# The dt projection as one 48-column stationary, laid out again by selection matmuls

## The chip, the cores and the metric

The kernel runs on one core of one Trainium2 chip. A core has five engines that work side by side and wait for each other only through semaphores: TensorE (PE in the profile, its weight loads PEld), VectorE (DVE), ScalarE (ACT), GpSimd (POOL) and SyncE (SP), which here issues DMAs. Times are microseconds of one execution on the device, from three timed runs; a separate profiled execution gives the trace.

## The reference

The reference is one layer of a hybrid decoder on 512 positions of width 1024: a mixer (16 Mamba-2 SSD heads of dimension 64 and pooled channel groups that share one input projection), cross-attention into 256 memory tokens, and a SwiGLU network, each behind an RMS norm. Only the head's step sizes matter here, all in float32:

```
proj = rmsnorm(x) @ w_in
z, xbc, dt_raw, v = split(proj)                 # dt_raw: 512 positions x 16 heads
dt   = softplus(dt_raw + dt_bias)
adt  = dt * (-exp(a_log))                       # per chunk of 128 positions, 4 chunks
a_cs = cumsum(adt, within the chunk)
seg  = exp(a_cs[l] - a_cs[s])  where l >= s     # in y_diag = (C B^T * seg) (xs * dt)
decay_states = exp(a_cs[last] - a_cs)           # states = B^T (decay_states * xs * dt)
chunk_decay  = exp(a_cs[last])                  # carries the state from chunk to chunk
```

Each position of a head thus needs three numbers: `dt`, `a_cs`, and `dt * decay_states`, the last two once the running sum of the chunk is there.

## The kernel before

Activations lie transposed, features on the 128 partitions and the 512 positions along the free dimension. A projection works on weight units of 128x1024 floats (eight blocks of 128x128 for one block of 128 output features). Each float32 operand is split into a high part, rounded to the format in which TensorE multiplies in one pass (ACT, `whi`, `t_xgh`, `t_uh`), and the low rest (DVE, `wlo`, `t_xgl`, `t_ul`); a product is three matmuls, high by high, high by low, low by high (`mm3`, lines 117 to 119). SP loads the units from HBM into six buffers (`raw`), ACT casts them into four (`whi`), DVE subtracts into five (`wlo`). A cast of a new unit therefore waits for the last matmul that reads the unit four earlier.

`SPEC` is a list of slots; a slot's items issue their matmuls together, with the preparation of the next slot, the follow-up of the slot before, and the casts of coming weights around them. In the first slot (`i_start`) all orders are those of the text; from the second slot on, the framework's scheduler fixes the order of every engine's instructions when the program is built. Engines execute in that order, so an instruction that waits holds up all that stand behind it on its engine.

The first slot projects the raw input, scaled by the norm's gain, for the step sizes (unit 0, PSUM tile `s`) and two blocks of convolution channels (units 1 and 2, also `s`); string `START_MM` lists them as unit and k-block. Token `r` in it is the matmul of the sum of squares (`r<-t_xacc,ones`, line 301), after which the norm's factor `t_r1t` is computed and the projections are multiplied by it.

For `dt` the 16 columns of the weight stand three times in a block of 96 (at 0, 32 and 64), so that the projection comes out three times on PSUM partitions 0 to 95. `i_dt` runs the whole chain on 96x512: Abs, Exp, Ln for softplus (lines 428 to 446), the multiplication by minus `exp(a_log)`, and one scan over 512 positions (line 450) whose multiplier `smask` is zero at the start of each chunk. Rows 32 to 47 of the scan go to DRAM (`d_acs`), from where each head's row is later read back to all partitions (`t_abc`, `t_E`); the four last values of each head go out as `d_last` and come back broadcast as `dl`, of which ACT makes `decb`, the chunk decays. Three copies (`dt`, `a_cs`, and the product with the decay) are gathered in `t_Tt` and turned by four transposes of 96x128 in item `tk` (`tokT`), which gives `tok`, positions on partitions.

Other items the text speaks of: `n:k` makes the normalised input's block k (`t_x`, then `t_uh` and `t_ul`), needed from `x:6` and `z:0` on; `x` and `z` are projections (matmuls into `xbc` and `z`; conv taps in `t_cv`); `t:g.c` transposes convolved channels (`xst`) and multiplies them by `dt` (`t_xc`) and by the decayed `dt` (`t_xd`), each split into high (`t_xch`, `t_xdh`, ACT) and low; `s:g.c` multiplies `t_xd` by the transposed B (`t_btmh`) into the state of a chunk (`st`).

Of the kernel before, what the change touches and what calls it, by code (L numbers as in the profile page):

```python
# [61 lines left out]
def hybrid_block(ctx: ExitStack, tc: tile.TileContext, a: dict, out: bass.AP,  # L62
# [185 lines left out]
    add_unit("dt", a["w_dt"], KT * 96)  # L248
# [90 lines left out]
    def i_start(its):  # L339
        it = Item(keys=["dt"] + [k for i in its[1:] for k in i.keys])  # L340

        def prep():
# [16 lines left out]
            for kind, i in [(t[0], int(t[1])) for t in start.split()]:  # L359
# [4 lines left out]
                elif kind in "hH":  # L364
# [7 lines left out]
                    split_into(hi[:, c], lo[:, c], raws[i][:, c])  # L372
# [7 lines left out]
        def mm():  # L380
# [37 lines left out]
    def i_dt():  # L418
        it = Item()

        def post():
            yield from need("r1")
            ps = it.ps
            r = st["r1",]
            R = slice(0, 96)
            bias = col(V_DTB, R)
            xr = T("dtx")
            nc.vector.tensor_tensor(out=xr[R], in0=ps[R], in1=r[R], op=ALU.mult)
            ax = T("dta")
            nc.scalar.activation(ax[R], xr[R], AF.Abs, bias=bias)  # L430
            nc.vector.tensor_scalar(out=xr[R], in0=xr[R], scalar1=bias, scalar2=0.0, op0=ALU.add, op1=ALU.max)
            e = T("dte")
            nc.scalar.activation(e[R], ax[R], AF.Exp, scale=-1.0)
            na = SM("na", [P, 1])
            nc.scalar.activation(na[R], col(V_ALOG, R), AF.Exp)
            yield
            u = T("dtu")
            nc.vector.tensor_scalar(out=u[R], in0=e[R], scalar1=1.0, scalar2=None, op0=ALU.add)
            l = T("dtl")
            nc.scalar.activation(l[R], u[R], AF.Ln)  # L440
            yield
            nc.vector.scalar_tensor_tensor(out=e[R], in0=u[R], scalar=1.0, in1=e[R],
                                           op0=ALU.subtract, op1=ALU.subtract)
            nc.vector.tensor_tensor(out=l[R], in0=l[R], in1=e[R], op=ALU.subtract)
            dt = T("dt")
            nc.vector.tensor_tensor(out=dt[R], in0=l[R], in1=xr[R], op=ALU.add)
            adt = T("adt")
            nc.vector.tensor_scalar(out=adt[R], in0=dt[R], scalar1=na[R], scalar2=-1.0, op0=ALU.mult, op1=ALU.mult)
            acs = T("acs")
            nc.vector.tensor_tensor_scan(acs[R], smask[R], adt[R], 0.0, ALU.mult, ALU.add)  # L450
            d_acs = dram.tile([H, S], F32, name="d_acs")
            d_last = dram.tile([H, NC], F32, name="d_last")
            last = SM("last", [P, NC])
            nc.vector.tensor_copy(last[R], acs[R].rearrange("p (c l) -> p c l", l=P)[:, :, P - 1])
            nc.sync.dma_start(d_acs, acs[32:48, :])
            nc.sync.dma_start(d_last, last[32:48, :])
            st["d_acs"] = d_acs
            dl = const.tile([P, H * NC], F32, name="dl")
            nc.sync.dma_start(dl, d_last.rearrange("h c -> (h c)").unsqueeze(0).broadcast_to([P, H * NC]))
            decb = const.tile([P, H, NC], F32, name="decb")  # L460
            yield
            Tt = T("Tt")
            nc.scalar.copy(Tt[0:32], dt[0:32])
            nc.scalar.copy(Tt[32:64], acs[32:64])
            ex = T("ex")
            for c in range(NC):
                cs = slice(c * P, (c + 1) * P)
                nc.scalar.activation(ex[64:96, cs], acs[64:96, cs], AF.Exp, scale=-1.0,
                                     bias=last[64:96, c:c + 1])
            nc.vector.tensor_tensor(out=Tt[64:96], in0=ex[64:96], in1=dt[64:96], op=ALU.mult)  # L470
            st["decay"] = decb, dl.rearrange("p (h c) -> p h c", c=NC)
            st["Tt"] = Tt

        it.post = post
        return it

    def i_tok():
        it = Item()

        def mm():  # L480
            pt = hold(it, "tokT")
            for c in range(NC):
                nc.tensor.transpose(pt[:, c * 96:(c + 1) * 96], st["Tt"][0:96, c * P:(c + 1) * P],
                                    ident[0:96, 0:96])

        def post():
            tok = const.tile([P, NC, 96], F32, name="tok")
            nc.vector.tensor_copy(tok.rearrange("p c h -> p (c h)"), it.ps[:, 0:NC * 96])
            st["tok"] = tok
# [72 lines left out]
    def i_tokens(g, c):  # L562
# [8 lines left out]
        def post():  # L571
# [5 lines left out]
            for key, off in zip(keys, (0, 64)):  # L577
# [933 lines left out]
```

## Time and profile before

| | |
|---|---|
| three timed runs | 794.51, 794.70, 795.65 us |
| median | 794.7 us |
| span of the profiled execution (first to last instruction) | 793.5 us |
| median less that span | 1.2 us |
| mean granted TensorE clock | 0.996 |
| idle time of DVE, ACT in the span | 20%, 37% |

The profiled execution is told by its span alone; what lies around it is taken from the difference to the median. In a row of a timeline stand the start, the duration, the engine, the line of the kernel, the operation, what it writes and reads, its shape and count, and in brackets the idle time before it and what ended that. Matmuls overlap in the pipeline: a duration of 0.39 us with the next start 0.23 us later costs 0.23 us. A matmul of true float32 operands, whose rows have no high or low part in their names, is recorded as two instructions, a transpose as one.

### The profile page before, as it was taken

The page shows a single profiled execution, that of the slowest core. Times are in us where ns is not written, and L with a number is a line of the kernel's source. Part 1 is how long each engine was busy: PE and PEld are TensorE (multiplying, and loading weights), DVE is VectorE, ACT ScalarE, POOL GpSimd, SP SyncE. Part 2 cuts the span into 40 slices and gives each one's busy share as a digit, 9 for nine tenths or more (in the row PEclk, how much of TensorE's full clock was granted, in tenths as well). Part 3 has the DMA queues.
Part 4 walks back from the last instruction along what each step waited for, and adds up shares of the span by engine and source line. Part 5 has one row for each costly group of instructions (what it writes and reads, how often), then busy time and mean ns, then how long its engine had stood idle before and what let it go on. Part 6 is the DMA issues. An engine that isn't in the chain of part 4 may idle for free.

```text
span 793.5 us, 10440 instructions
## 1 busy us (share of the span) xinstructions
PE 782.1 (99%) x3780; PEld 655.1 (83%) x3780; DVE 635.8 (80%) x945; ACT 498.4 (63%) x799; POOL 49.9 (6%) x66
## 2 busy tenths in 40 slices
PE   9999999999999999999999999999999999999995
PEld 7888888888888888888888888888888888888984
DVE  7999879999885799875766667788867698868897
ACT  8667699557953547555655695665445575455845
POOL 0000000000000000000000001011101011101000
PEclk9999999999999999999999999999999999999998
DMA  9235225133475234775446268688879697869602
GB/s 331 91 112 184 109 82 179 54 111 122 162 257 171 84 107 150 170 198 163 134 116 153 60 154 222 171 243 166 239 157 291 163 251 172 245 154 272 165 14 106
DMA packets 41282, 128.60 MB, mean 162 GB/s; under 512 B 4864, under 2 KB 7296, under 8 KB 41232
## 3 DMA queue, kind: packets, MB, share of 16 engines
q1 hardware_dynamic: 33024, 99.30, 37.0%
q0 software_dynamic: 8064, 28.58, 20.1%
q8 instruction: 29, 0.48, 0.2%
q14 instruction: 21, 0.17, 0.1%
q10 hardware_dynamic: 144, 0.07, 0.1%
HBM read 116.63 MB, written 2.13 MB: 150 GB/s over the span
## 4 chain that ended last, share of the span: by engine, by line
PE 92%; DVE 5%; issue 1%; DMA 1%; ACT 0%; SPq 0%; DVEq 0%
PE gA L1102 15%; PE gB L1102 8%; PE dA L1102 5%; PE gC L1102 4%; PE dB L1102 2%; PE xbc L117 2%; PE xbc L119 2%; PE xbc L118 2%; PE vAB L1102 2%; PE k L889 2%; PE z L117 2%; PE z L119 2%; PE op L117 2%; PE z L118 2%; PE wo L119 2%; PE op L118 2%
## 5 line engine op out<-in xcount | busy, mean ns | idle before, releaser
L203 ACT CAST whi<-raw 128x1024 fp32r<-128x1024 f32 (+1 forms) x125 | 129.0, 1040 | 91.1 <-PE wo L118 11.8
L205 DVE TENSOR_TENSOR wlo<-raw,whi 128x1024 fp32r<-128x1024 f32 (+1 forms) x125 | 149.8, 1208 | 28.2 <-ACT whi L203 27.3
L203 ACT CAST whi<-wq 128x1024 fp32r<-128x1024 f32 (+1 forms) x76 | 77.4, 1028 | 74.6 <-PE dA L1102 17.8
L205 DVE TENSOR_TENSOR wlo<-wq,whi 128x1024 fp32r<-128x1024 f32 (+1 forms) x76 | 90.3, 1194 | 38.7 <-ACT whi L203 38.6
L172 POOL DMA_DIRECT2D raw<-w_s x38 | 32.8, 867 | 646.0 <-DMA raw<-w_s 486.4
L1102 PE MATMUL gA<-whi,t_xh 128*128 128x512 f32 (+1 forms) x192 | 71.8, 374 | 0.0
L1102 PE MATMUL gA<-wlo,t_xh 128*128 128x512 f32 (+1 forms) x192 | 71.4, 372 | 0.0
L1102 PE MATMUL gA<-whi,t_xl 128*128 128x512 f32 (+1 forms) x192 | 71.3, 371 | 0.0
L1102 PEld LDWEIGHTS gA<-whi,t_xh 128*128 128x128 f32 x192 | 36.2, 188 | 6.6 <-ACT whi L203 0.4
L1102 PEld LDWEIGHTS gA<-wlo,t_xh 128*128 128x128 f32 x192 | 36.2, 188 | 6.3
L1102 PEld LDWEIGHTS gA<-whi,t_xl 128*128 128x128 f32 x192 | 36.2, 188 | 6.1
L1118 ACT ACTIVATE t_gu<-t_gu,s 128x512 f32<-128x512 f32 (+1 forms) x24 | 16.4, 688 | 35.9 <-DVE t_gu L1114 35.8
L194 DVE TENSOR_TENSOR wq<-wq,wq 128x1024 f32<-128x1024 f32 (+1 forms) x19 | 22.5, 1194 | 17.7 <-DMA wq<-raw 17.7
L1102 PE MATMUL dA<-whi,t_xh 128*128 128x512 f32 x88 | 34.1, 392 | 0.3 <-DVE t_hT L1259 0.2
L1102 PE MATMUL dA<-whi,t_xl 128*128 128x512 f32 x88 | 34.3, 389 | 0.0
L1102 PE MATMUL dA<-wlo,t_xh 128*128 128x512 f32 x88 | 34.1, 389 | 0.0
L1102 PE MATMUL gB<-whi,t_xq 128*128 128x512 f32 (+1 forms) x96 | 27.5, 371 | 0.0
L1180 ACT CAST t_xh<-t_x 128x512 fp32r<-128x512 f32 x30 | 18.6, 621 | 10.6 <-DVE t_x L1199 6.4
L117 PE MATMUL wo<-t_oh,whi 128*128 128x512 f32 x64 | 25.2, 394 | 0.0
L117 PE MATMUL v<-t_uh,whi 128*128 128x512 f32 x64 | 25.1, 392 | 0.0
L117 PE MATMUL z<-t_uh,whi 128*128 128x512 f32 x64 | 25.1, 392 | 0.0
L117 PE MATMUL q<-t_hgh,whi 128*128 128x512 f32 x64 | 25.1, 392 | 0.0
(401 smaller groups left out, 2221.2 us busy)
## 6 DMA issues: line engine op xcount, KB each, us to landing
raw<-w_u SPq DMA_DIRECT2D x68, 512.0 KB, 3.4
raw<-w_s SPq DMA_DIRECT2D x54, 512.0 KB, 4.6
wq<-w_s SPq DMA_DIRECT2D x36, 512.0 KB, 5.9
raw<-w_s POOLq DMA_DIRECT2D x36, 512.0 KB, 7.5
wq<-raw POOLq DMA_DIRECT2D x17, 512.0 KB, 8.6
t_x<-xT SPq DMA_DIRECT2D x16, 256.0 KB, 5.4
t_abc<-d_acs SPq DMA_DIRECT2D x16, 256.0 KB, 4.6
out<-t_hT SPq DMA_DIRECT2D x8, 256.0 KB, 2.3
```

The source lines that it names most:

```text
L117: nc.tensor.matmul(ps, whi, xhi, start=start, stop=False)
L118: nc.tensor.matmul(ps, whi, xlo, start=False, stop=False)
L119: nc.tensor.matmul(ps, wlo, xhi, start=False, stop=stop)
L172: nc.gpsimd.dma_start(sw[c, f][:, :n], quad("11" if f == 7 else "22"), accum_op=ALU.add)
L194: add = nc.vector.tensor_tensor(out=sw[c, 3][:, :n], in0=sw[c, 3][:, :n], in1=sw[c, 6][:, :n], op=ALU.add)
L203: nc.scalar.copy(hi[:, :n], raw[:, :n])
L205: nc.vector.tensor_tensor(out=lo[:, :n], in0=raw[:, :n], in1=hi.bitcast(F32)[:, :n], op=ALU.subtract)
L889: nc.tensor.matmul(it.ps[d], wh[:, ws], both, start=k == 0, stop=False, skip_group_check=True)
L1102: nc.tensor.matmul(it.ps[tt], p[:, ts_], w[:, ws], start=first, stop=(c, i, n) == pairs[-1] and p is xh and w is wl, skip_group_check=True)
L1118: st["silu"] = nc.scalar.activation(g, g, AF.Silu, scale=st["r3",][:, c:c + 1])
L1180: nc.scalar.copy(h if w is None else h[:, w], src)
```

## The change

The weight of `dt` becomes a block of 48 columns: the high part at columns 0 to 15, the low part at 32 to 47, zeros between. Two passes, with the high and the low part of the input, then form all four products; their results lie on PSUM partitions 0 to 15 and 32 to 47. The first multiplication by `t_r1t` stays where it was (`t_dtx`, now 48x512). A new item `ds`, in a slot of its own after `x:3`, adds the two groups of rows and spreads the chunks over the partitions: for each chunk one float32 matmul with a 48x128 matrix of zeros and ones (`pick`, made on POOL), so that heads of chunk c stand on partitions 32c to 32c+15 and positions within the chunk along the free dimension (`dts`, 128x128). The chain for softplus, scan and decay runs on 128x128; the scan needs no restarts. `d_last` is now one value for each of 128 partitions, `d_acs` is written in four pieces, `dl` is 128x128. Three transposes of 128x128 give `tok`, whose indices change with the users of `tok` and `decb`. The mask `smask`, the copies into `t_Tt` and the copy `last` go.

```diff
-    "x:2", "x:3 n:0 n:1 n:2 n:3", "x:4", "n:4 n:5 n:6", "n:7", "x:5 z:0", "x:8 x:6",
+    "x:2", "x:3 n:0 n:1 n:2 n:3", "ds", "x:4", "n:4 n:5 n:6", "n:7", "x:5 z:0", "x:8 x:6",
...
-    smask = T("smask")
-    nc.gpsimd.memset(smask, 1.0)
-    nc.gpsimd.memset(smask.rearrange("p (c l) -> p c l", l=P)[:, :, 0:1], 0.0)
+    pick = T("pick").rearrange("p (c r) -> p c r", r=P)
+    nc.gpsimd.memset(pick, 0.0)
+    for c in range(NC):
+        for base in (0, 32):
+            nc.gpsimd.affine_select(out=pick[:, c, 32 * c:32 * c + H], in_=pick[:, c, 32 * c:32 * c + H],
+                                    compare_op=ALU.not_equal, fill=1.0, base=-base, pattern=[[-1, H]],
+                                    channel_multiplier=1)
...
-                    split_into(hi[:, c], lo[:, c], raws[i][:, c])
+                    if i == 0:
+                        nc.scalar.copy(hi[:, c], raws[i][:, c])
+                        h3 = hi[:, c].rearrange("p (k n) -> p k n", n=48)
+                        nc.vector.tensor_tensor(out=h3[:, :, 32:48],
+                                                in0=raws[i][:, c].rearrange("p (k n) -> p k n", n=48)[:, :, 32:48],
+                                                in1=h3.bitcast(F32)[:, :, 0:H], op=ALU.subtract)
+                    else:
+                        split_into(hi[:, c], lo[:, c], raws[i][:, c])
...
-                n = (96, P, P)[u]
+                n = (48, P, P)[u]
                 whi, wlo = ready[it.keys[u]]
+                if u == 0:
+                    for h in range(2):
+                        nc.tensor.matmul(pss[u][0:n, :], whi[:, k * n:(k + 1) * n], st["xg"][k][h],
+                                         start=k == 0 and h == 0, stop=k == KT - 1 and h == 1)
+                    continue
...
+    def i_dtsum():
+
+        it = Item()
+
+        def mm():
+            ps = hold(it, "dts")
+            for c in range(NC):
+                nc.tensor.matmul(ps[:, 0:P], pick[0:48, c, :], st["dtx"][0:48, c * P:(c + 1) * P],
+                                 start=c == 0, stop=c == NC - 1)
+
+        def post():
+            ps = it.ps[:, 0:P]
+            bias = col(V_DTB)
+            t = T("dta"), T("dtu")
+            ax, e, xr, u = [t[0][:, o:o + P] for o in range(0, 512, P)]
+            l, adt, ex, one = [t[1][:, o:o + P] for o in range(0, 512, P)]
+            nc.vector.memset(one, 1.0)
+            nc.scalar.activation(ax, ps, AF.Abs, bias=bias)
+            nc.vector.tensor_scalar(out=xr, in0=ps, scalar1=bias, scalar2=0.0, op0=ALU.add, op1=ALU.max)
+            nc.scalar.activation(e, ax, AF.Exp, scale=-1.0)
...
+            nc.vector.tensor_scalar(out=u, in0=e, scalar1=1.0, scalar2=None, op0=ALU.add)
+            nc.scalar.activation(l, u, AF.Ln)
...
+            nc.vector.tensor_scalar(out=adt, in0=dt, scalar1=na, scalar2=-1.0, op0=ALU.mult, op1=ALU.mult)
+            nc.vector.tensor_tensor_scan(acs, one, adt, 0.0, ALU.mult, ALU.add)
+            last = acs[:, P - 1:P]
+            d_acs = st["d_acs"] = dram.tile([H, S], F32, name="d_acs")
+            d_last = dram.tile([P, 1], F32, name="d_last")
+            nc.sync.dma_start(d_last, last)
             for c in range(NC):
+                nc.sync.dma_start(d_acs[:, c * P:(c + 1) * P], acs[32 * c:32 * c + H])
+            dl = T("dl", n=P).rearrange("p (c h) -> p c h", h=32)
+            nc.sync.dma_start(dl.rearrange("p c h -> p (c h)"), d_last.rearrange("r o -> o r").broadcast_to([P, P]))
+            nc.scalar.activation(ex, acs, AF.Exp, scale=-1.0, bias=last)
+            yield
+            nc.vector.tensor_tensor(out=wdt, in0=ex, in1=dt, op=ALU.mult)
+            st["decay"] = const.tile([P, NC, 32], F32, name="decb"), dl
...
-            for c in range(NC):
-                nc.tensor.transpose(pt[:, c * 96:(c + 1) * 96], st["Tt"][0:96, c * P:(c + 1) * P],
-                                    ident[0:96, 0:96])
+            for n in range(3):
+                nc.tensor.transpose(pt[:, n * P:(n + 1) * P], st["D3"][:, n * P:(n + 1) * P], ident)
```

The scheduler sets the order anew. Three places of it are shown; from the first state matmuls on, about a tenth into TensorE's rows, its order is the same as before.

First, ACT ahead of the last block of the normalised input. In the kernel before, `t_uh` rows are the casts of that input, `decb` the chunk decays, `t_ex` the decay of the positions:

```order
L464 COPY t_Tt_392<-t_acs_369 32x512
L468 ACT_TABLE_LOAD
L468 ACTIVATE t_ex_395<-t_acs_369,last_373 32x128 x4
L506 ACTIVATE t_cv_428<-t_xr_426,vec 128x512
L414 ACTIVATE decb<-dl 128x64
L506 ACTIVATE t_cv_467<-t_xr_465,vec 128x512
L233 CAST t_uh_476<-t_x_118 128x512
L233 CAST t_uh_478<-t_x_124 128x512
L233 CAST t_uh_480<-t_x_112 128x512
```

With the change, on the same engine:

```order
L469 ACT_TABLE_LOAD
L469 ACTIVATE t_dtu_457<-t_dta_456 128x128
L237 CAST t_uh_471<-t_x_147 128x512
L237 CAST t_uh_473<-t_x_135 128x512
L207 CAST whi_627<-raw_538 128x1024
L486 ACT_TABLE_LOAD
L486 ACTIVATE t_dtu_457<-t_dt_93_477 128x128
L430 ACTIVATE decb<-t_dl_488 128x128
L522 ACTIVATE t_cv_526<-t_xr_524,vec 128x512
L237 CAST t_uh_533<-t_x_145 128x512
```

Before, the chain's first Exp and its Ln stood further up among functions of one table set, and four casts of the input came behind `decb`. Now the Ln (the first two rows) and the decay's Exp have table loads of their own, as has the first Exp further up, and of the casts only that of the eighth block, `t_uh_533`, stands behind `decb`, with one convolution function between.

Second, SP at the chain's DMAs. With the change:

```order
L481 DMA d_last<-t_dt_93_477 128x1
L483 DMA d_acs<-t_dt_93_477 16x128 x4
L485 DMA t_dl_488<-d_last 128x128
L184 DMA raw_641<-w_u 128x1024
L184 DMA raw_825<-w_u 128x1024
```

Before, `d_acs` (one DMA) came first, then `d_last` and `dl`, and the weight loads behind them as here.

Third, ACT ahead of the first state matmul. Before (`t_xdh_842` is what `st` reads; the `whi` rows are casts of coming weights):

```order
L233 CAST t_cth_832<-t_cv_805 128x512
L233 CAST t_xch_840<-t_xc_811 128x512
L233 CAST t_xdh_842<-t_xd_813 128x512
L203 CAST whi_1046<-raw_815 128x1024
L512 ACTIVATE t_cv_807<-t_cv_807 128x512
L506 ACTIVATE t_cv_915<-xbc_861,vec 128x512
L600 COPY t_prev_917<-st_886 128x512
```

With the change (`t_xdh_852` is what `st` reads):

```order
L237 CAST t_cth_842<-t_cv_815 128x512
L207 CAST whi_1056<-raw_825 128x1024
L237 CAST t_xch_850<-t_xc_821 128x512
L237 CAST t_xdh_852<-t_xd_823 128x512
L528 ACTIVATE t_cv_817<-t_cv_817 128x512
L522 ACTIVATE t_cv_925<-xbc_871,vec 128x512
L616 COPY t_prev_927<-st_896 128x512
```

The weight cast has moved ahead of the two casts of the tokens.

More of the change, by code (lines that the diff above doesn't have):

```diff
@@ L422, in post @@
             yield from need("r1")
[L423 to L433, printed above, removed]
+            xr = st["dtx"] = T("dtx")
@@ new lines, in post @@
+            nc.vector.tensor_tensor(out=xr[0:48], in0=it.ps[0:48], in1=st["r1",][0:48], op=ALU.mult)
+        it.post = post
+        return it
+    def i_dtsum():
[15 more added lines that the diff above has]
+            nc.scalar.activation(e, ax, AF.Exp, scale=-1.0)
@@ L434, in post @@
             na = SM("na", [P, 1])
-            nc.scalar.activation(na[R], col(V_ALOG, R), AF.Exp)
+            nc.scalar.activation(na, col(V_ALOG), AF.Exp)
             yield
[L437 to L440, printed above, removed]
+            nc.vector.tensor_scalar(out=u, in0=e, scalar1=1.0, scalar2=None, op0=ALU.add)
+            nc.scalar.activation(l, u, AF.Ln)
@@ L441, in post @@
             yield
[L442 to L457, printed above, removed]
@@ L458, in post @@
-            dl = const.tile([P, H * NC], F32, name="dl")
-            nc.sync.dma_start(dl, d_last.rearrange("h c -> (h c)").unsqueeze(0).broadcast_to([P, H * NC]))
-            decb = const.tile([P, H, NC], F32, name="decb")
-            yield
[L462 to L465, printed above, removed]
-            for c in range(NC):
-                cs = slice(c * P, (c + 1) * P)
-                nc.scalar.activation(ex[64:96, cs], acs[64:96, cs], AF.Exp, scale=-1.0,
-                                     bias=last[64:96, c:c + 1])
@@ L470, in post @@
[L470 to L474, printed above, removed]
+            nc.vector.scalar_tensor_tensor(out=e, in0=u, scalar=1.0, in1=e, op0=ALU.subtract, op1=ALU.subtract)
+            nc.vector.tensor_tensor(out=l, in0=l, in1=e, op=ALU.subtract)
+            D = st["D3"] = T("dt3")
+            dt, acs, wdt = [D[:, o:o + P] for o in range(0, 384, P)]
@@ new lines, in post @@
+            nc.vector.tensor_tensor(out=dt, in0=l, in1=xr, op=ALU.add)
+            nc.vector.tensor_scalar(out=adt, in0=dt, scalar1=na, scalar2=-1.0, op0=ALU.mult, op1=ALU.mult)
[4 more added lines that the diff above has]
+            nc.sync.dma_start(d_last, last)
+            for c in range(NC):
+                nc.sync.dma_start(d_acs[:, c * P:(c + 1) * P], acs[32 * c:32 * c + H])
@@ L481, in mm @@
             pt = hold(it, "tokT")
-            for c in range(NC):
-                nc.tensor.transpose(pt[:, c * 96:(c + 1) * 96], st["Tt"][0:96, c * P:(c + 1) * P],
-                                    ident[0:96, 0:96])
+            for n in range(3):
+                nc.tensor.transpose(pt[:, n * P:(n + 1) * P], st["D3"][:, n * P:(n + 1) * P], ident)
         def post():
-            tok = const.tile([P, NC, 96], F32, name="tok")
-            nc.vector.tensor_copy(tok.rearrange("p c h -> p (c h)"), it.ps[:, 0:NC * 96])
+            tok = const.tile([P, 3, NC, 32], F32, name="tok")
+            nc.vector.tensor_copy(tok.rearrange("p n c h -> p (n c h)"), it.ps[:, 0:3 * P])
             st["tok"] = tok
@@ L576, in post @@
             srcs = []
-            for key, off in zip(keys, (0, 64)):
+            for key, n in zip(keys, (0, 2)):
                 t = T(key[0])
-                w = tok[:, c, off + 8 * g:off + 8 * g + 8].unsqueeze(2).broadcast_to([P, 8, 64])
+                w = tok[:, n, c, 8 * g:8 * g + 8].unsqueeze(2).broadcast_to([P, 8, 64])
                 nc.vector.tensor_tensor(out=t.rearrange("p (h d) -> p h d", d=64), in0=pv, in1=w, op=ALU.mult)
@@ L601, in post @@
             else:
-                d = st["decb"][:, 8 * g:8 * g + 8, c:c + 1].broadcast_to([P, 8, 64])
+                d = st["decb"][:, c, 8 * g:8 * g + 8].unsqueeze(2).broadcast_to([P, 8, 64])
                 nc.vector.tensor_tensor(out=f.rearrange("p (h d) -> p h d", d=64),
@@ L647, in prep @@
                         nc.scalar.activation(D[:, cs], abc[:, cs], AF.Relu, scale=-1.0,
-                                             bias=tok[:, c, 32 + h:33 + h])
+                                             bias=tok[:, 1, c, h:h + 1])
                     else:
-                        nc.vector.tensor_scalar(out=D[:, cs], in0=abc[:, cs], scalar1=tok[:, c, 32 + h:33 + h],
+                        nc.vector.tensor_scalar(out=D[:, cs], in0=abc[:, cs], scalar1=tok[:, 1, c, h:h + 1],
                                                 scalar2=0.0, op0=ALU.subtract, op1=ALU.min)
@@ L1466, in _pack @@
                 w_s[c, q, :, n * j:n * j + n] = src()
-    dtp = np.zeros((KT, P, 96), z32)
-    for r in range(3):
-        dtp[:, :, 32 * r:32 * r + 16] = wdt.reshape(KT, P, 16)
-    w_dt = f(dtp.transpose(1, 0, 2).reshape(P, KT * 96))
+    dtp = np.zeros((KT, P, 48), z32)
+    for o in (0, 32):
+        dtp[:, :, o:o + 16] = wdt.reshape(KT, P, 16)
+    w_dt = f(dtp.transpose(1, 0, 2).reshape(P, KT * 48))
     vecs = np.zeros((P, V_N), z32)
@@ L1488, in _pack @@
     put(V_DSK, np.repeat(g["d_skip"], 64))
-    for r in range(3):
+    for r in range(NC):
         vecs[32 * r:32 * r + 16, V_DTB] = g["dt_bias"]
```

5 lines of the change are left out of this document (3 added, 2 removed).

## The prediction

> **What bounds the kernel now.** I read the page's busy shares and its chain of waits first, then the list of TensorE's waits, and then the timelines of the four engines over the first 95 us, where all that changes lies.
>
> ```profile
> PE 782.1 (99%) x3780; PEld 655.1 (83%) x3780; DVE 635.8 (80%) x945; ACT 498.4 (63%) x799; POOL 49.9 (6%) x66
> ...
> PE 92%; DVE 5%; issue 1%; DMA 1%; ACT 0%; SPq 0%; DVEq 0%
> ```
>
> ```profile
> PE warm L384 <- DVE ones L100: 1.2, 1, 1.2
> PE s L117 <- ACT whi L130: 0.8, 1, 0.8
> PE yo L119 <- DVE t_prl L241: 0.4, 1, 0.4
> PE dA L1102 <- DVE t_hT L1259: 0.2, 1, 0.2
> ```
>
> TensorE is busy for 99% of the span, and its waits (total, times, longest) sum to 2.6 us, 2.0 of them before 8 us. It sets the end. So a removed TensorE instruction counts in full as long as its successors have their operands, and a new wait counts in full too, since hardly any idle time comes later that could take it up. Work removed from DVE and ACT counts only where it lets TensorE go on sooner.
>
> **The change part by part. Third passes removed.**
>
> ```profile
> 1.18 5.17 PE L384 MATMUL warm<-ones 128*128 128x128 f32 x24 [1.18 <-DVE ones L100]
> ...
> 11.01 0.39 PE L117 MATMUL s<-t_xgh,whi 128*96 128x512 f32 x1
> 11.24 0.39 PE L118 MATMUL s<-t_xgl,whi 128*96 128x512 f32 x1
> 11.47 0.40 PE L119 MATMUL s<-t_xgh,wlo 128*96 128x512 f32 x1
> ...
> 18.01 1.04 PE L301 MATMUL r<-t_xacc,ones 128*128 128x512 f32 x2
> ```
>
> ```profile
> 7.20 1.03 ACT L130 CAST whi<-raw 128x512 fp32r<-128x512 f32 x2 [0.58 <-DMA raw<-w_u]
> ```
>
> ```profile
> 6.03 0.56 DVE L131 TENSOR_TENSOR wlo<-raw,whi 128x384 fp32r<-128x384 f32 x1 [0.17 <-ACT whi L130]
> 7.84 1.16 DVE L131 TENSOR_TENSOR wlo<-raw,whi 128x512 fp32r<-128x512 f32 x2 [0.44 <-ACT whi L130]
> 16.39 1.48 DVE L324 TENSOR_TENSOR t_xacc<-t_xacc,t_sq 128x512 f32<-128x512 f32 x2
> ```
>
> ```profile
> 5.00:10.00 5.00, 4.25 (x19) 2.94 (x19) 4.22 (x7) 4.42 (x10) 0.00 (x0) 1.00 0.98 327
> ```
>
> A pass starts 0.23 us after the one before, whatever its columns, so eight of them are worth 1.84 us. Five (blocks 0 to 4) lie before the matmul r, 1.15 us, and three, 0.69, behind it. Behind r I take all of the 0.69. Before r TensorE can't simply move up: r reads `t_xacc`, which DVE ends at 16.39 + 1.48 = 17.87, after rows that follow each other without idle time from 7.84 on. That stretch shrinks by the second half of the low part: 0.56 becomes a subtraction of 64 columns, which I price below by 0.16 (the copy of 4 columns quoted further down) and take at 0.2, so 0.36 less. It also begins sooner, as it waits for ACT's cast at 7.20, which waits for a weight DMA; the DMA share in that window is 0.98 at 327 GB/s, and 96 KB less ahead of it are 0.3 us by bytes, nothing if the count of packets decides. So r moves up by 0.36 to 0.66; I take the upper end, since the bytes are halved. Together 0.66 + 0.69 = **1.35 us gained**; bounds 0.36 + 0.69 = 1.05 and 1.84.
>
> **Selection matmuls and transposes.** From the chain of waits (start, length):
>
> ```profile
> 18.17 0.88 PE r L301 x2
> 68.79 0.33 PE tokT L483 x4
> 69.12 0.44 PE xst L569 x4
> ```
>
> No row shows a 48x128 float32 matmul. The nearest is r, float32 with 512 columns, 0.88; a quarter of the columns is 0.22, and four are **0.88 us added**. Below, four at the pace of the 128-column transposes are 0.44. Above, the warm-up matmuls with 128 columns took 5.17 us for twelve (24 records), 1.7 for four, at the very start of the span. I take 0.88, as r ran in the same state as its neighbours. Three transposes of 128 columns at 0.11 cost the 0.33 that four of 96 cost: nothing.
>
> **The chain on 128x128, and who stands behind it.** The rows of before:
>
> ```profile
> 44.41 0.16 DVE L454 COPY last<-t_acs 96x4 f32<-96x4 f32 x1
> 50.65 4.22 DVE L509 SCALAR_TENSOR_TENSOR t_cv<-t_xr,vec,t_cv 128x511 f32<-128x511 f32 x6
> 45.09 2.48 DVE L241 TENSOR_TENSOR t_ul<-t_x,t_uh 128x512 fp32r<-128x512 f32 x4
> 40.03 1.21 DVE L205 TENSOR_TENSOR wlo<-raw,whi 128x1024 fp32r<-128x1024 f32 x1
> 23.01 2.08 DVE L406 SCALAR_TENSOR_TENSOR t_x<-t_x,vec,t_r1t 128x512 f32<-128x512 f32 x3
> ```
>
> ```profile
> 44.60 0.31 SPq L456 DMA_DIRECT2D d_last<-last  x1
> 47.58 0.34 SPq L459 DMA_DIRECT2D dl<-d_last  x1
> ```
>
> ```profile
> 50.48 0.26 ACT L414 ACTIVATE decb<-dl 128x64 f32<-128x64 f32 x1 [0.32 <-DMA dl<-d_last]
> 50.64 0.80 ACT L506 ACTIVATE t_cv<-t_xr,vec 128x512 f32<-128x512 f32 x1
> 58.04 0.60 ACT L233 CAST t_uh<-t_x 128x512 fp32r<-128x512 f32 x1
> ```
>
> ```profile
> 59.55 0.39 PE L117 MATMUL z<-t_uh,whi 128*128 128x512 f32 x1
> 60.46 0.39 PE L118 MATMUL z<-t_ul,whi 128*128 128x512 f32 x1
> ```
>
> The chain's instructions get a quarter as wide, but it starts only behind `x:3`, and its end decides when ACT passes `decb`, behind which the eighth block of the normalised input is now cast. When? In the new order DVE has between the norm factor and the scan 8 input scalings and 12 taps (0.67 each by the rows with x3 and x6), 11 of 0.6 (six low parts, five products with the factor), 6 weight subtractions (1.13 start to start) and seven small ones at 0.2: 13.4 + 6.6 + 6.8 + 1.4 = 28.2 us, from 23.01 - 0.66 on: 50.5. The Ln before it waits on ACT behind two table loads, 0.6 more, and the scan of 128 columns takes a quarter of 1.2: it ends at about 51.5, against 43.9 before. `d_last` to `dl` took 44.60 to 47.58 and `dl` to `decb` 47.58 to 50.48, 5.9 us in all, so `decb` starts at 57.4; with 0.16 for it and 0.7 for the conv function behind it (start to start), the cast runs from 58.3 to 58.9. TensorE wants the block where it wanted it at 59.55, less what it gained: 59.55 - 1.35 + 0.88 = 59.1; the low half, at 60.46 - 0.47 = 60.0, comes about 59.8. So what was off the path arrives just in time, and every tenth of lateness counts. What could make it late: 128 rows of 4 bytes in place of 16 rows of 16, and four more issues before `dl`. Bounds 0 and 1.5 us (5.9 grown by a quarter); I take **0.3 us added**.
>
> Table loads: the row of before costs its own length and no more, since the next function starts right after it:
>
> ```profile
> 33.93 1.28 ACT L512 ACT_TABLE_LOAD   x1 [1.12 <-DVE t_cv L509]
> 35.22 1.28 ACT L512 ACTIVATE t_cv<-t_cv 128x512 f32<-128x512 f32 x2
> ```
>
> [...]
>
> The rest costs nothing: the sequences on POOL run in its idle time before the 34 us at which `pick` is needed; weight loads queued on SP behind `dl` are used at 80 us and later; `t_abc`, loaded at 58 us before, is read by no one until past 100.
>
> **The new wait at the first state matmul.**
>
> ```profile
> 84.46 0.62 ACT L233 CAST t_xch<-t_xc 128x512 fp32r<-128x512 f32 x1
> 84.98 0.62 ACT L233 CAST t_xdh<-t_xd 128x512 fp32r<-128x512 f32 x1
> 86.62 1.06 ACT L203 CAST whi<-raw 128x1024 fp32r<-128x1024 f32 x1 [1.01 <-PE xbc L118]
> 87.58 0.62 ACT L512 ACTIVATE t_cv<-t_cv 128x512 f32<-128x512 f32 x1
> ```
>
> ```profile
> 86.19 0.39 PE L118 MATMUL xbc<-t_ul,whi 128*128 128x512 f32 x1
> 86.42 0.39 PE L119 MATMUL xbc<-t_uh,wlo 128*128 128x512 f32 x1
> 86.64 0.39 PE L117 MATMUL st<-t_xdh,t_btmh 128*128 128x512 f32 x1
> ```
>
> The weight cast at 86.62 waited for the last-but-one matmul of `x:10` (86.19), for its buffer. The state matmul stands two places behind that one. Before, its operand had been cast at 84.98. Now `t_xch` and `t_xdh` stand behind the weight cast, with the same wait. From the start of that matmul: 0.43 until the cast starts, 0.96 to the next ACT instruction, 0.52 to the one after, 0.62 for it, 0.04 to signal: 2.57, where TensorE needs the operand after 0.45. **2.12 us added**, whatever happened earlier. Bounds: 0 if the cast should not have to wait, 2.6 if the low half is late too.
>
> **Sum.** -1.35 + 0.88 + 0.30 + 2.12 = +1.95 us. The profiled span of 793.5 us becomes 795.45, and with the 1.2 us between it and the median **796.7 us**, 0.25% more. A measurement of this kernel can tell about 0.2%, 1.6 us, from no change, so "slower" begins at 796.3.
>
> **The rivals.**
>
> *No wait at the state matmul* (the other side). If the weight cast finds its buffer free when ACT reaches it, the tokens are cast in time and the gain of the start stays: -1.35 + 0.88 = -0.47, 794.2 us. It is decided by whether ACT's idle time before that cast is gone. Against it: that cast idled 1.01 us for TensorE before, and the buffers are as many. 9%.
>
> *A better start.* If DMA and DVE let all eight passes count and the eighth block is on time: -1.84 + 0.88 + 2.12 = +1.16, 795.9 us. For it: the waits before r are tenths of a us. Against: DVE is full from 7.84 to r. 13%.
>
> *The chain decides at the z matmuls.* If the small DMAs take a quarter longer, the block is 1.5 late: -0.47 + 1.5 + 2.12 = +3.15, 797.9 us. For it: no spare time by my sum. 17%.
>
> *The clock falls in the pause.* The twelve warm-up matmuls took 0.43 each, twice r's 0.22; a fall to that pace for as long as it lasted at the start would cost half of 5.17, 2.6 us: 799.3. Against it: after the 0.8 us wait of `s` for `whi` the matmuls (11.01 on) stand 0.23 apart. 3%. [...]
>
> **How the numbers follow.** The forecast's own case gets 55%, from 796.0 to 797.2 by the width of its start and of the eighth block's lateness; 40 of the 55 lie above 796.3. With 17 and 3, slower is 0.60. The remaining 15, the better start's 13 and 8 of the first rival make 0.36 within 0.2%. Faster gets 0.04, one point of that rival and 3 for what I have not seen. For 8 in 10 the range leaves out the first rival below and the clock, with the far part of the late chain, above: 795.3 to 798.0.
>
> **What would show it.** In the profile after, TensorE's waits should list `st` for ACT's `t_xdh` with about 2.1 us, and r should start near 17.4. `dts` should take 0.9 us on the chain. `z` for ACT's `t_uh` should show a few tenths, `decb` should start near 57 to 58. DVE and ACT should lose some us of busy time with no effect on the end. The prediction is wrong if the wait at `st` is missing, if z waits for over 1 us, or if matmuls behind a pause run at half pace.

## The result, and the profile after

The changed kernel takes 809.7 us (median of four runs, 807.5 to 810.1) against 794.9 us. The ratio, formed from the single runs and not from the two medians, is 1.0178 (95% interval 1.0166 to 1.0190). It is slower, as forecast, but by 14.8 us and not by 2, far outside the range. The profiled execution has a span of 808.3 us, 14.8 more than before.

The page and the list of TensorE's waits in the changed kernel (total, times, longest):

```profile
PE 786.4 (97%) x3779; PEld 657.2 (81%) x3779; DVE 633.0 (78%) x945; ACT 500.2 (62%) x797; POOL 51.7 (6%) x73
...
PE 88%; DVE 6%; DMA 2%; ACT 2%; issue 1%; SPq 0%; DVEq 0%
```

```profile
PE z L121 <- ACT t_uh L237: 7.5, 1, 7.5
PE st L121 <- ACT t_xdh L237: 2.0, 1, 2.0
PE s L121 <- ACT whi L134: 1.2, 1, 1.2
```

DMA has come into the chain of waits, and two new waits stand at the top. They make 9.5 us. TensorE's busy time has grown by 4.3 us as well, though it has fewer matmul columns to do: at the granted clock of 0.50, shown further down, matmuls start 0.43 us apart in place of 0.23. What z waited for shows on SP, on ACT and in the DMA issues (the last number is the time from issue to landing):

```profile
53.90 0.33 SPq L481 DMA_DIRECT2D d_last<-t_dt  x1
...
63.16 0.34 SPq L485 DMA_DIRECT2D t_dl<-d_last  x1
```

```profile
66.65 0.31 ACT L430 ACTIVATE decb<-t_dl 128x128 f32<-128x128 f32 x1 [10.51 <-DMA t_dl<-d_last]
...
67.57 0.60 ACT L237 CAST t_uh<-t_x 128x512 fp32r<-128x512 f32 x1
```

```profile
d_acs<-t_dt SPq DMA_DIRECT2D x4, 8.0 KB, 8.9
...
d_last<-t_dt SPq DMA_DIRECT2D x1, 0.5 KB, 9.2
```

In the kernel before, the same view has for the smaller write

```profile
d_last<-last SPq DMA_DIRECT2D x1, 0.2 KB, 3.0
```

The write of 128 values of 4 bytes takes 9.2 us, three times as long as the 16 rows of 16 bytes. `decb` waits 10.5 us for the round trip, and the cast of the eighth block, two places behind it on ACT, is made at 67.6 where TensorE wants it at 60.6. `decb` itself is first read by DVE at 112.1 us.

The busy time by stretches shows the second loss (start:end, length, TensorE's busy time and instructions, granted clock, DMA share, GB/s):

```profile
64.00:68.00 4.00, 0.00 (x0) 0.50 0.44 147
68.00:74.00 6.00, 5.77 (x14) 0.50 0.00 0
...
98.00:101.40 3.40, 1.55 (x7) 1.00 0.47 151
101.40:104.80 3.40, 3.40 (x10) 0.50 0.22 47
```

Behind each of the two waits the granted clock is 0.50 for a while (63.8 to 74.1 and 101.4 to 104.8 us), and matmuls start 0.43 us apart. TensorE's timeline at the places on which the accounts below rest:

```profile
34.99 0.39 PE L123 MATMUL xbc<-t_xgh,wlo 128*128 128x512 f32 x1
35.30 1.16 PE L452 MATMUL dts<-t_dtx,t_pick 48*128 48x128 f32 x8
36.39 0.50 PE L121 MATMUL xbc<-t_xgh,whi 128*128 128x512 f32 x1
...
60.33 0.39 PE L121 MATMUL xbc<-t_uh,whi 128*128 128x512 f32 x1
68.23 0.79 PE L121 MATMUL z<-t_uh,whi 128*128 128x512 f32 x1 [7.51 <-ACT t_uh L237]
68.82 0.63 PE L122 MATMUL xbc<-t_ul,whi 128*128 128x512 f32 x1
69.24 0.63 PE L123 MATMUL xbc<-t_uh,wlo 128*128 128x512 f32 x1
...
74.24 0.40 PE L122 MATMUL xbc<-t_ul,whi 128*128 128x512 f32 x1
...
97.51 0.39 PE L123 MATMUL xbc<-t_uh,wlo 128*128 128x512 f32 x1
99.84 0.50 PE L121 MATMUL st<-t_xdh,t_btmh 128*128 128x512 f32 x1 [1.95 <-ACT t_xdh L237]
...
104.99 0.39 PE L122 MATMUL st<-t_xdl,t_btmh 128*128 128x512 f32 x1
```

Counted from start to start, with 0.23 us as the normal distance:

| place | working | us |
|---|---|---|
| up to the selection matmuls | 34.99 + 0.23 = 35.22, where `xbc` of the next slot stood at 35.98 before | -0.76 |
| selection matmuls | 36.39 - 35.22 | +1.17 |
| wait of z | 68.23 - 60.33 - 0.23 | +7.67 |
| half pace behind it | 14 distances from 68.23 to 74.24, less 14 x 0.227 | +2.83 |
| wait of st | 99.84 - 97.51 - 0.23 | +2.10 |
| half pace behind it | 15 distances from 99.84 to 104.99, less 15 x 0.227 | +1.74 |
| sum | the spans differ by 14.8 | +14.75 |

### The profile page after: what moved, and what is told of

Same layout as the page of the kernel before. It is cut to its first block, busy times and chain, and to the rows that moved or that the text cites. A ratio compares the mean times of both kernels' runs of the same rounds, so it can differ in the third digit from the quotient of the medians.

```text
span 808.3 us, 10451 instructions
## 1 busy us (share of the span) xinstructions
PE 786.4 (97%) x3779; PEld 657.2 (81%) x3779; DVE 633.0 (78%) x945; ACT 500.2 (62%) x797; POOL 51.7 (6%) x73
## 4 chain that ended last, share of the span: by engine, by line
PE 88%; DVE 6%; DMA 2%; ACT 2%; issue 1%; SPq 0%; DVEq 0%
PE gA L1118 15%; PE gB L1118 7%; PE dA L1118 5%; PE gC L1118 4%; PE dB L1118 2%; PE vAB L1118 2%; PE k L905 2%; PE op L121 2%; PE wo L123 2%; PE op L122 2%; PE q L121 2%; PE wo L122 2%; PE wo L121 2%; PE os L122 2%; PE q L123 2%; PE op L123 2%
## 5 line engine op out<-in xcount | busy, mean ns | idle before, releaser
L123 PE MATMUL z<-t_uh,wlo 128*128 128x512 f32 x64 | 25.9, 405 | 0.0
L122 PE MATMUL z<-t_ul,whi 128*128 128x512 f32 x64 | 25.8, 403 | 0.0
L1196 ACT CAST t_xh<-t_x 128x512 fp32r<-128x512 f32 x30 | 18.7, 623 | 10.5 <-DVE t_x L1215 6.4
```

Source lines behind the costliest of these rows:

```text
L122: nc.tensor.matmul(ps, whi, xlo, start=False, stop=False)
L123: nc.tensor.matmul(ps, wlo, xhi, start=False, stop=stop)
L1196: nc.scalar.copy(h if w is None else h[:, w], src)
```

## The experiments

The first question was what made the write slow: its form (128 rows of 4 bytes), or the queue it shares with the weight loads ahead of it and the four pieces of `d_acs` behind it. The second was whether the rest of the loss follows from that write. The third was the half pace, which the second wait shows though it lasts only 2 us. Each ratio is to the kernel before in the same comparison.

**The same 512 bytes in 16 rows.** All orders stay as in the changed kernel.

```diff
-            d_last = dram.tile([P, 1], F32, name="d_last")
-            nc.sync.dma_start(d_last, last)
+            d_last = dram.tile([16, 8], F32, name="d_last")
+            nc.sync.dma_start(d_last, acs[0:16, P - 8:P])
...
-            nc.sync.dma_start(dl.rearrange("p c h -> p (c h)"), d_last.rearrange("r o -> o r").broadcast_to([P, P]))
+            nc.sync.dma_start(dl.rearrange("p c h -> p (c h)"), d_last.rearrange("r o -> (r o)").unsqueeze(0).broadcast_to([P, P]))
```

> The changed kernel, but d_last is filled from 16 partitions with 8 floats each (the last 8 positions of 16 rows) instead of 128 partitions with 1 float each: the same 512 bytes in 16 rows, everything else and every order as in the changed kernel (the decays of the chunks are then wrong values). Theory 'rows of 4 bytes': the write takes as long as it has rows, 3.0 us for the 16 rows of before and 9.2 us for 128, so here about 3.0; decb then starts 6.2 us earlier (60.4 instead of 66.65), z waits about 1.3 us in place of 7.5, and the 13 matmuls at half pace behind z (2.7 us) run at full pace: 809.7 - 6.2 - 2.7 = 800.8 us, or 799.2 if the half pace behind st (1.7 us) is gone too. Rival 'queue' (the write waits for the weight loads ahead of it or the four pieces of d_acs behind it, which are all still there): it lands after 9 us again and the time stays at 809.7.

798.3 us, 1.0044 (1.0027 to 1.0061). The issues, then TensorE's waits:

```profile
d_acs<-t_dt SPq DMA_DIRECT2D x4, 8.0 KB, 1.4
...
d_last<-t_dt SPq DMA_DIRECT2D x1, 0.5 KB, 1.8
```

```profile
PE st L121 <- ACT t_xdh L237: 1.9, 1, 1.9
...
PE z L121 <- ACT t_uh L237: 0.6, 1, 0.6
```

The write lands after 1.8 us, with the weight loads and the pieces where they were. So it isn't the queue: the pieces, which took 8.9 us behind the write of 9.2, take 1.4 behind this one. The time is below both that were expected, since the write took 1.8 us and not 3.0. The form of one DMA of half a KB is worth 11.4 us of the 809.7. In the profiled executions 1.7 of that is the half pace behind `st`, which didn't follow here behind the same wait of 1.95 us; the last section shows what differed.

**64 rows of 8 bytes.** As above with `[64, 2]` and `acs[0:64, P - 2:P]`.

> As rows16, but 64 rows of 2 floats (the chunk decays are wrong values). Theory 'rows of 4 bytes', with (9.2 - 3.0) / 112 = 0.055 us for each row: the write lands after 3.0 + 48 x 0.055 = 5.7 us, z waits 4.0 us, the time is 809.7 - 3.5 = 806.2 us if the matmuls behind z still run at half pace, 803.5 if they don't. Rival 'queue': 9.2 us and 809.7. It also tells whether a pause of about 4 us is enough for the half pace.

805.7 us, 1.0133 (1.0113 to 1.0154). The write lands after 4.1 us, z waits 4.2 us, and the half pace stays behind both waits:

```profile
62.45:69.25 6.80, 4.80 (x11) 0.50 0.13 50
...
96.55:99.95 3.40, 3.40 (x9) 0.50 0.00 0
```

16, 64 and 128 rows take 1.8, 4.1 and 9.2 us: 0.05 us for each row at first, 0.08 behind that. In this series the rows also get shorter (32, 8 and 4 bytes), so these are no prices of a row alone. z still waits 4.2 where 4.0 was expected, although the write was 1.6 us quicker than expected: `dl` took 5.2 us here, 3.5 with the 128 rows below.

**128 rows of 512 bytes.**

```diff
+            d_last = dram.tile([P, P], F32, name="d_last")
+            nc.sync.dma_start(d_last, acs)
...
+            nc.sync.dma_start(dl.rearrange("p c h -> p (c h)"), d_last[0:1, :].broadcast_to([P, P]))
```

> The changed kernel, but d_last is written as 128 rows of 512 bytes (the whole scan, 64 KB) and dl reads the first of these rows (the chunk decays are wrong values). If the number of rows sets the time of the write whatever they hold, it lands after 9.2 us as before and the kernel takes 809.7 us. If it is the shortness of the rows, it lands like the weight loads of 128 rows, within 3.5 us, and the kernel takes about 800 us as with rows16. Rival 'queue': 9.2 us.

799.6 us (two executions, 798.2 and 800.9), 1.0056 (1.0034 to 1.0078). 128 times as many bytes land in 2.0 us, where 128 rows of 4 bytes took 9.2:

```profile
d_last<-t_dt SPq DMA_DIRECT2D x1, 64.0 KB, 2.0
```

So it is neither the number of rows by itself nor the bytes, but many rows that are short. Whether reading 4 bytes from each partition takes the time, or writing them side by side into HBM, no run separates. With 128 rows the write took 2.0 us at 512 bytes a row and 9.2 at 4; what lengths between them take, no run with 128 rows shows.

**The pieces behind it.** `dl` was written ahead of `d_acs` in the code.

> The changed kernel with one order changed: dl is issued ahead of the four pieces of d_acs. Theory 'rows of 4 bytes': d_last still lands 9.2 us after its issue and dl starts at 63 us as now, so z waits 7.5 us and the time is 809.7 us. Rival 'queue, the pieces behind it': without them in the queue d_last lands after some 3 us, decb comes 6 us earlier and the time is near 800 us.

809.9 us, 1.0186 (1.0165 to 1.0206), but the scheduler put the issue of `dl` behind the pieces again, so this was a second run of the changed kernel and says nothing of the order. It shows how much the slow write varies: 11.0 us here, 9.2 there.

**One row of ACT moved.** `decb` behind the eighth cast instead of ahead of it; the slow write stays.

```diff
...
-                nc.scalar.activation(st["decb"], dl, AF.Exp)
+                after(nc.scalar.activation(st["decb"], dl, AF.Exp), st["ucast"])
```

> The changed kernel with one row of ACT moved: decb stands behind the cast of the eighth block instead of two places ahead of it; the slow write of 128 rows of 4 bytes and all else stay. Theory (the loss came from the cast that stood behind the round trip): the cast is made at 57 to 58 us and z doesn't wait; decb still waits until 66.7 us and now holds up the weight cast and the conv functions behind it, which with 16 rows ran from 62.5 to 66 us and are wanted by the transposes xst at about 70: a wait of 1 to 3 us there, too short for the half pace in most executions. Time 797.4 (16 rows without their wait at z) + 2 = 799.4 us, between 798.4 and 801. Rival (what else stands behind the slow write, the weight loads held on SP until 63.6 us, costs as much): no gain, 807 us or above.

805.8 us, 1.0130 (1.0113 to 1.0147): between the two. z doesn't wait any more, so its loss did come from the cast that stood behind `decb`. But the wait went on to what now stands behind it, the functions of the conv that the transposes read:

```profile
68.50 0.31 ACT L432 ACTIVATE decb<-t_dl 128x128 f32<-128x128 f32 x1 [8.55 <-DMA t_dl<-d_last]
```

```profile
PE xst L587 <- ACT t_cv L530: 4.5, 2, 2.8
```

The theory had the place right and the size wrong (4.5 in place of 1 to 3): the write took 11.4 us in this execution, and the granted clock was 0.50 here too, behind this wait (73.5 to 80.4) and behind that of `st` (97.4 to 100.9). Moving the reader of a slow round trip two places down on ACT didn't cure it here: the wait of 7.5 us at z became 4.5 at `xst`.

**No round trip at all.** The last values are spread by a matmul:

```diff
-            nc.sync.dma_start(d_last, last)
...
+            nc.vector.tensor_scalar(out=lb, in0=ones, scalar1=last, scalar2=float(DM), op0=ALU.mult, op1=ALU.mult)
...
+            nc.tensor.matmul(ps[:, 0:P], st["lb"], ident, start=True, stop=True)
+            nc.scalar.activation(st["decb"].rearrange("p c h -> p (c h)"), it.ps[:, 0:P], AF.Exp)
```

> The changed kernel with the last values of the chunks spread over the partitions by one float32 128x128 matmul (item db behind the transposes of tok, its stationary made by one DVE instruction) in place of d_last and dl; decb's Exp reads PSUM. In the order that the scheduler then makes, the casts t_xch and t_xdh stand ahead of the weight cast again. Theory (the loss of the changed kernel is the round trip of decb, the wait at st, and the half pace behind both): no wait at z, none at st, no half pace; what is left against before is -0.76 us of the start (as in the trace of the changed kernel up to the selection matmuls), +1.17 for the selection and about +0.25 for the new matmul, so +0.7: 795.6 us with 794.9 for before. Rival 'the chain on 128x128 with its three table loads is late in itself': z still waits for t_uh, by a us or more, 797 us or above.

796.5 us, 1.0020 (1.0011 to 1.0029). The waits at z and at st are gone, and the clock stays at 1.00 there. What is left is 0.6 us above the sum. The profiled execution, the slowest of the eleven (797.8), shows a new wait; how much of it the others have isn't known:

```profile
69.27 1.28 ACT L677 ACT_TABLE_LOAD   x1 [1.64 <-DMA t_E<-d_acs]
...
70.99 0.26 ACT L497 ACTIVATE decb<-db 128x128 f32<-128x128 f32 x1
```

```profile
71.31 0.50 PE L121 MATMUL xbc<-t_uh,whi 128*128 128x512 f32 x1 [1.14 <-ACT decb L497]
```

`decb` now stands on ACT behind the Exp of `t_E`, which waits for another DMA, and a matmul waits for `decb`, presumably for the PSUM tile that it reads. 128-wide chain and selection matmuls, without the round trip, still leave the kernel 0.2% slower.

**The forecast's wait at st, alone.** Five and eight idle copies on ACT ahead of the casts of the first tokens in the kernel before:

```diff
...
+            if (g, c) == (0, 0):
+                for _ in range(5):
+                    pad = nc.scalar.copy(T("pad"), srcs[-1])
...
```

> The kernel before with five more ACT copies of 128x512 ahead of the casts t_xch and t_xdh of the first tokens (their results are read by no one), so that the first state matmul waits about 2.1 us; all else as before. It prices the wait of the forecast by itself. If a wait costs its length: 794.9 + 2.1 = 797.0 us in every execution. If a wait that fills more than half of one of the stretches of 3.41 us, by which the granted clock changed in the traces so far (at 63.9, 74.1, 101.4 and 104.8 us with the change, at 62.5, 69.3, 96.6 and 100.0 with 64 rows), halves the clock for the next stretch, then executions whose stretch holds 1.85 us or more of the wait take 1.7 us longer, and the others not: two groups, near 797.0 and near 798.7. [...]

> As pad5 with eight copies, so that the wait is about 3.7 us. If a wait costs its length: 794.9 + 3.7 = 798.6 us. By the rule of half a stretch of 3.41 us, one of the stretches always holds 1.85 us of this wait, so every execution has at least one stretch at half the clock behind it, 1.7 us of loss: 800.3 us or above, and the profile shows the granted clock at 0.50 for 3.4 us. [...]

798.5 us with five, 1.0042 (1.0029 to 1.0055), the executions from 797.5 to 799.2; 800.3 with eight, 1.0069 (1.0057 to 1.0080), from 799.3 to 802.6. In the profiled executions the granted clock was 0.50 behind the shorter wait (2.0 us) and stayed at 1.00 behind the longer one (3.5 us). Five copies:

```profile
86.00:88.15 2.15, 0.20 (x1) 1.00 0.00 0
88.15:91.55 3.40, 3.38 (x8) 0.50 0.06 16
```

Eight copies:

```profile
86.90:90.40 3.50, 0.00 (x0) 1.00 0.00 0
90.40:93.80 3.40, 3.40 (x15) 1.00 0.05 8
```

So the length of a wait didn't decide here. That a wait costs its length alone falls with five copies. That a wait of eight copies always costs the clock, as I had written, falls too: it was 3.5 us long, not 3.7. What the falls went with is in the last section. Five copies didn't give two clear groups of times; the kernel before itself spreads over 2.3 us in that comparison.

**The two passes alone.** DVE adds rows 32 to 47 to rows 0 to 15, and the chain of before runs on 16x512; no selection matmuls, no 128 rows.

```diff
+            nc.vector.tensor_tensor(out=xr[0:48], in0=ps[0:48], in1=r[0:48], op=ALU.mult)
+            nc.vector.tensor_tensor(out=xr[R], in0=xr[R], in1=xr[32:48], op=ALU.add)
...
```

> One part of the change alone: the 48-column stationary and the two passes, but no selection matmuls; DVE adds rows 32 to 47 to rows 0 to 15 (one instruction 16x512), and the chain of the kernel before runs on 16x512, with its DMAs (16 rows) and its four transposes of 96. Theory (two passes are worth what the start of the changed kernel gained, and the rest of the change only costs): 794.9 - 0.76 = 794.1 us, down to 793.1 if all eight passes count. Rival (the extra DVE instruction delays the taps and the normalised input, as DVE is full from 8 to 60 us): a new wait at z of 0.5 us or more, 794.7 to 795.5 us, no gain.

794.7 us, 0.9993 (0.9984 to 1.0001): not to be told from no change. The forecast rival came true: z waits 0.5 us for the low half, which DVE makes, and takes back a part of what the start gained.

```profile
PE z L118 <- DVE t_ul L241: 0.5, 1, 0.5
```

**DVE relieved.** First by GpSimd, for two instructions of the chain:

> As two2 (two passes, DVE adds the rows, the old chain on 16x512), with two instructions of the chain, the last subtraction for the logarithm and the sum that makes dt (16x512 each), on GpSimd in place of DVE. Theory (in two2 the gain at the start, 0.8 us, was taken back by the wait of z for the low half that DVE made 0.5 us late, as DVE is full): DVE is 1.2 us ahead at 46 us, z doesn't wait, and the time is 794.7 - 0.7 = 794.0 us, 0.15% under before. Rival (GpSimd's instructions on 512 columns take several us and hold up the scan, so that decb or the transposes of tok come late): a new wait of TensorE between 50 and 70 us, 795 us or above.

797.4 us, 1.0028 (1.0017 to 1.0039), for the reason the rival gave, only earlier: the first of the two took 6.58 us, the second 1.27, and DVE stood behind them, so that z waited 2.4 us; behind that wait the granted clock was 0.50 for one stretch (48.0 to 51.4).

```profile
35.46 6.58 POOL L457 TENSOR_TENSOR t_dtl<-t_dtl,t_dte 16x512 f32<-16x512 f32 x1 [33.05 <-DVE t_dte L455]
42.12 1.27 POOL L459 TENSOR_TENSOR t_dt<-t_dtl,t_dtx 16x512 f32<-16x512 f32 x1
```

Then by ACT:

```diff
-            nc.vector.tensor_scalar(out=xr[R], in0=xr[R], scalar1=bias, scalar2=0.0, op0=ALU.add, op1=ALU.max)
+            nc.scalar.activation(xr[R], xr[R], AF.Relu, bias=bias)
...
-            nc.vector.tensor_scalar(out=adt[R], in0=dt[R], scalar1=na[R], scalar2=-1.0, op0=ALU.mult, op1=ALU.mult)
+            nc.scalar.activation(adt[R], dt[R], AF.Identity, scale=na[R])
...
```

> As two2 (two passes, DVE adds rows 32 to 47 to rows 0 to 15, the old chain on 16x512, no selection matmuls), with two DVE instructions of the chain on ACT instead: the maximum with zero (a Relu with bias) and the product with exp(a_log) (the scan subtracts). Theory (DVE, which is full from 8 to 60 us, took the gain back through the wait of z): DVE is 0.9 us ahead at 46 us, the wait of z goes from 0.5 us to under 0.2, and the time is 794.7 - 0.5 = 794.2 us, 0.1% under before, for which the interval must lie below 1. Rival (ACT is late with the two, or its casts behind them are): a wait of TensorE for ACT between 30 and 60 us, and 795 us or more.

794.1 us, 0.9988 (0.9979 to 0.9997): 0.12% faster than the kernel before. The interval ends just below 1, and this was the third variant tried for the gain, so it is a small effect on thin evidence. The wait for DVE's low half is gone; 0.4 us for ACT's high half stand in its place, more than the 0.2 expected:

```profile
PE z L117 <- ACT t_uh L233: 0.4, 1, 0.4
```

## Why the prediction was wrong, point by point

**The step that failed** is the one on who stands behind the chain. It had the mechanism: `decb` waits for the round trip, the eighth cast stands behind `decb`, z needs it without any spare time, and 128 rows of 4 bytes were named as what could make it late. But the write was priced with the row of 16 rows, 3.0 us, and its bound was "5.9 grown by a quarter", which no row carried. The write took 9.2, and 0.30 us (bounds 0 and 1.5) became 7.67, of which 0.75 stayed when the write was quick. The same row gave another bound: eight times the rows, eight times 3.0, with which the range would have reached past 810. Nor was the 3.0 a clean price for 16 rows: that write was issued 0.67 us behind `d_acs`, which took 3.4, so that they landed at 47.3 and 47.6; issued ahead of `d_acs`, a write from 16 rows took 1.8.

**The second step that failed** is the rival of the clock, at 3%, held off by a wait of 0.8 us that hadn't cost the clock. What a wait of 2 us does, the trace of before didn't show; that it wouldn't cost the clock was the author's estimate. The fall happened twice, for 2.83 and 1.74 us. The first followed from the long wait; the second came behind exactly the wait that was forecast, though it doesn't always come there. That rival's price, half of the warm-up's 5.17, lies between the two.

**Without the slow write the time would have lain in the range, but not on its terms.** With 16 rows, whose write was quicker (1.8 us) than the 3.0 of the forecast, the kernel took 3.0 us more than before (798.3 against 795.4), where 1.95 was the sum. Its terms in the profiled execution of that run, where the clock didn't fall:

| term | forecast | measured |
|---|---|---|
| start | -1.35 | -1.09 |
| selection matmuls | +0.88 | +1.18 |
| eighth block at z | +0.30 | +0.75 |
| first state matmul | +2.12 | +2.10 |

```profile
34.66 0.39 PE L123 MATMUL xbc<-t_xgh,wlo 128*128 128x512 f32 x1
34.98 1.16 PE L452 MATMUL dts<-t_dtx,t_pick 48*128 48x128 f32 x8
36.07 0.50 PE L121 MATMUL xbc<-t_xgh,whi 128*128 128x512 f32 x1
...
60.00 0.39 PE L121 MATMUL xbc<-t_uh,whi 128*128 128x512 f32 x1
60.98 0.50 PE L121 MATMUL z<-t_uh,whi 128*128 128x512 f32 x1 [0.59 <-ACT t_uh L237]
...
87.52 0.39 PE L123 MATMUL xbc<-t_uh,wlo 128*128 128x512 f32 x1
89.85 0.50 PE L121 MATMUL st<-t_xdh,t_btmh 128*128 128x512 f32 x1 [1.95 <-ACT t_xdh L237]
```

The start is 34.66 + 0.23 = 34.89 against 35.98, the selection 36.07 - 34.89, the other two from start to start less 0.23.

*Start.* One pair of executions says little here. The place that stands at 35.98 in the kernel before lies at 35.38 and 36.05 in the two other traces with the old start (five and eight copies), so the -0.76 and -1.09 are uncertain by some tenths. The first 128x512 cast of a weight, expected 0.3 us sooner than 7.20 by the halved bytes, came at 7.30 in the changed kernel, at 6.67 to 7.02 in the nine other traces with the 48-column stationary, and at 7.20, 7.26 and 6.47 with the old one: whether the bytes set that landing isn't shown. Matmul r came at 17.77 instead of 17.4, and at 17.13 to 17.48 in those nine. What the forecast had wrong is what follows. TensorE reached its wait of `s` for `whi` one pass sooner and waited longer there, 1.19 us instead of 0.75 (0.87 with 16 rows), so that the first of the eight passes gained little or nothing. And r was not what the norm's factor waited for: ACT makes it behind a table load and two casts of the input, 12.05 us after that first cast of a weight (7.30 to 19.36; 6.91 to 18.96 with 16 rows), whenever r comes. The chain thus began at 22.97 (22.56 with 16 rows), where I had put 23.01 - 0.66 = 22.35.

```profile
18.12 1.34 ACT L137 ACTIVATE t_xgh<-t_x,vec 128x512 fp32r<-128x512 f32 x2
19.36 0.67 ACT L310 ACTIVATE t_r1y<-r,eps 128x512 f32<-128x512 f32 x1
```

*Selection.* Eight records at about 0.15 (1.17 and 1.18 in the two runs), between the bounds 0.44 and 1.7, and above the taken 0.88.

*The chain.* `decb` started at 59.4 with the quick write, 2 us after the 57.4 of the sum. The scan ended at 53.5 instead of 51.5: DVE idled 0.4 and 1.1 us for ACT on its way, where 0.6 was taken; the rest isn't traced to a row. That z waited only 0.6 is due to TensorE being late too, by the two terms above and by two matmuls more that the new order puts ahead of the block (106 instead of 104). So the rival "the chain decides", with the block 1.5 late, was nearer in how late the chain was, and the forecast's own case was nearer in what it cost, which is luck.

*First state matmul.* Right in mechanism and size, 2.10 against 2.12 in both runs, and gone where the scheduler put the token casts ahead of the weight cast again (the matmul in place of the round trip).

What the list of waits shows is less than a wait costs: 0.59, 1.95 and 7.51 us there are 0.75, 2.10 and 7.67 from start to start, since the idle time is counted from the modelled end of a matmul, 0.39 after its start, where the next could have started after 0.23.

## What to carry to other kernels

The small write of these runs had its time from the length and the number of its rows, not from its bytes (512 bytes took 1.8 us in 16 rows and 9.2 in 128; 64 KB in 128 rows took 2.0): look at what each row holds on the partition side before a layout turns 16 rows into 128 single values, and give the write a bound that scales with the rows. Ask of every wait on an engine that executes in order what stands behind it, not what reads its result: `decb` wasn't needed for another 45 us, and its place cost 10 us, wait and half pace together. In this kernel, which keeps TensorE busy for 99% of the span, work saved there was worth only what DVE and ACT could follow: of 1.84 us of passes, 0.5 to 1 came through in the two variants without selection matmuls that kept the chain off GpSimd.

## What the runs showed of the hardware that was not expected

**Writes in short rows.** 512 bytes from 16, 64 and 128 partitions landed 1.8, 4.1 and 9.2 to 11.4 us after their issue, 64 KB from 128 partitions after 2.0, and the `d_acs` writes issued behind the one of 9.2 us landed 8.9 us after theirs, against 1.4 behind the one of 1.8.

**The clock's stretches.** Every trace records the times at which the granted clock changed. In all 13 the later changes lie whole multiples of 3.41 us after the first one: with the change at 5.8, 63.8, 74.1, 101.4 and 104.8; with 64 rows at 4.4, 62.4, 69.2, 96.6 and 100.0. With eight copies the first is at 6.7 and the next at 791.8, behind TensorE's last matmul, 230 stretches of 3.413 us later. Where this grid lies differs between executions (first changes at 5.8, 4.4 and 6.7 us here), so it cuts the waits of these runs in different places. For the longest waits, TensorE's idle time within one stretch (up to a matmul's start, from the modelled end of the one before) and the granted clock in the next stretch:

| run | wait | stretch | idle in it | next clock |
|---|---|---|---|---|
| 128 rows of 512 bytes | st, 1.9 | 88.5 to 91.9 | 1.26 | 1.00 |
| eight copies | st, 3.5 | 88.7 to 92.1 | 1.74 | 1.00 |
| 16 rows | st, 1.9 | 86.2 to 89.7 | 1.75 | 1.00 |
| eight copies | st, 3.5 | 85.2 to 88.7 | 1.78 | 1.00 |
| the change | st, 2.0 | 98.0 to 101.4 | 1.87 | 0.50 |
| 64 rows | st, 1.9 | 93.1 to 96.6 | 1.94 | 0.50 |
| five copies | st, 2.0 | 84.8 to 88.2 | 1.96 | 0.50 |
| two instructions on GpSimd | z, 2.4 | 44.6 to 48.0 | 2.10 | 0.50 |
| 64 rows | z, 4.2 | 59.0 to 62.4 | 2.16 | 0.50 |

All other stretches of the 13 traces fit, those at the end of the work too: with up to 1.78 us idle of the 3.41 the clock stayed, from 1.87 on it was 0.50 in the next one. So the falls in these traces went not with the length of a wait but with the idle time within one stretch, 1.87 us or more of 3.41; that the forecast's wait at st cost another 1.74 us in the changed kernel and nothing with 16 rows (1.87 and 1.75 us in one stretch) went with where the grid lay. The full clock came back after a stretch with 0.29 us idle or less, and not after those with 0.86 and 0.97 (`decb` moved, and the change, behind their long waits). This is read from traces of one kernel and its variants; no run set the grid's place on purpose. Whether the grid's place is also why executions of one kernel with such waits differ by 2 to 3 us (eight copies: 799.3 to 802.6) isn't shown.

**GpSimd's first arithmetic.** With two instructions of the chain on GpSimd, its first on two 16x512 operands took 6.58 us, the next 1.27.
